# Pairing the 64-row score products of latent attention and retention in the two halves of the TensorE array

## The chip, the cores and the metric

The kernel runs on one core of one Trainium2 chip. The metric is the time of one execution on the device, in microseconds (us); a run is one such time, and the time of a kernel is the median of its runs. The profile is that of one execution, and all its times are counted from the start of its span.

## What is computed

One layer of an encoder for 256 tokens of 1024 features, in float32. After a norm, a wide product with `w_in` feeds four mixers, whose outputs are projected, gated and summed; then come `w_out`, a feed-forward block and a gated projection. Mixers C and D are the ones that matter here:

```python
# C, latent attention: 8 heads; q and k have 128 plain features and 64 rotated ones; k's rotated part is shared
q = (_rms_norm(cq, qa_g) @ wuq).reshape(b, s, 8, 192);  kv = (_rms_norm(ckv, kva_g) @ wukv).reshape(b, s, 8, 256)
k_nope, v = kv[..., :128], kv[..., 128:]
a = softmax(einsum('bhqd,bhkd->bhqk', q, k) * 192 ** -0.5);  y = einsum('bhqk,bhke->bhqe', a, v)
# D, retention: 8 heads, q and k of 64 rotated features, scores times a decay, then a norm per head and a gate
scores = einsum('bhnid,bhnjd->bhnij', q, k) * decay;  y = silu(g) * head_layer_norm(scores @ v)
```

B, differential attention, also has products over 64 features: two score maps for each of its 8 heads.

## The kernel before, in words

Weights are streamed once through the core. Every matrix is split into a high and a low part (`hi` by ScalarE or VectorE, `lo` by VectorE), and each product is made of three matmuls: high by high, high by low, low by high (`mm3`, line 196). The stream (`a_mode`, line 387, and `b_mode`, line 416) loads chunks of up to 1 MB into `raw` (3 buffers, issued on SP's queue at line 362), splits them in pieces into `hi` and `lo` (5 buffers each), and multiplies into the four PSUM banks named `acc`.

The mixers' own work is "side work": Python generators that emit a step at a time between chunks of the stream (`tick`, line 333; at most four generators in turn, each as far as a credit of estimated cost goes). `yield` ends a step. All side work that needs TensorE shares four other PSUM banks, named `mm` (`mm_bank`, line 181): transposes (`pair_T`, line 580), scores and products with v. The framework orders the instructions of each engine at build time from the program's order, the dependences and its own estimate of durations, gives out the buffers, and sets the waits; each engine then runs its list in order.

`c_mix` (line 763) makes a pair of heads of C. After three steps of preparation the pair's operands are in place: `qn`, `kn` (128 rows, high and low, per head) and `pe` (the rotated 64 features: head 0 of the pair in partitions 0 to 63, head 1 in 64 to 127). Then `scores(h)` (line 793) takes one `mm` bank for a head and emits, for each of two tiles of 128 queries, three matmuls over 128 rows and three over 64 rows into the same columns, followed by the softmax: a row maximum and its product with `rq` on VectorE (lines 802, 803), two `Exp` with running sums on ScalarE (line 805), a reciprocal and two scalings on VectorE (lines 807, 809). Head 0 is one step, head 1 the next:

```python
e0 = scores(0)
yield 1.4
e1 = scores(1)
yield 1.4
```

`d_mix` (line 877) does the same for a pair of D: `scores(h)` (line 881) loads a decay table of 256 KB on SP's queue (line 883), makes six matmuls over 64 rows (two tiles of keys, three each) into one `mm` bank and multiplies it by the decay on VectorE (line 890). There are four pairs in C and four in D. `b_mix` (line 631) makes two maps of a head in one step: the comment at line 640 says that they run in the two halves of the array's rows, each into its own bank.

Of the kernel before, what the change touches and what calls it, by code (L numbers as in the profile page):

```python
# [10 lines left out]
AF = mybir.ActivationFunctionType  # L11
ALU = mybir.AluOpType
AX = mybir.AxisListType
# [6 lines left out]
# buffers of each kind of tile  # L20
NR, NY, NG, NL, NS = 5, 8, 4, 18, 16
# side work: generators in turn; its cost for a chunk of weights, by phase
WIDTH = 4
G0, G1, G2, G3 = 3.0, 3.0, 3.5, 2.5
# priority of weight loads and splits over what else is ready; of the first norm over everything
AHEAD, AHEAD_S, FIRST = 60, 60, 100000
# in these pieces of the stream VectorE makes every second high part, as ScalarE has more to do
# [6 lines left out]
# weight streams: (name, first row, rows, first column, columns, mode); a chunk of at most 1 MB is  # L34
# contiguous in each partition. "a": [k][n]; "b": [128-column tile][k][128].
# [61 lines left out]
# then, on every partition: gains of rotated columns [q/k][plain/halves swapped][16 | 64], diff_lam,  # L97
# and rope tables [tile of tokens][diff C 16 | S 16 | mla C 64 | S 64 | ret C 64 | S 64]
# [5 lines left out]
def _pack_params(w):  # L104
    """the small parameters, a column of 128 features or a row for all partitions each"""
    import numpy as np

    out = np.empty((P, N_PAR), np.float32)
    for name, k in _COLS:
        v = np.asarray(w[name][0])  # L110
        if name in ('diff_q_g', 'diff_k_g'):
            v = np.concatenate([np.ones(16, np.float32), v[16:]] * 2)
        elif name in ('mla_q_g', 'mla_k_g'):
            v = v[:P]
        out[:, _COL[name]:_COL[name] + k] = v.reshape(k, P).T
    rows = []
    for dn, mn in (('diff_q_g', 'mla_q_g'), ('diff_k_g', 'mla_k_g')):
        d, m = np.asarray(w[dn][0])[:16], np.asarray(w[mn][0])[P:]
        rows += [d, m, d[8:], d[:8], m[32:], m[:32]]
    rows.append(np.asarray(w['diff_lam'][0]).reshape(-1))  # L120
    out[:, O_GR:O_ROPE] = np.concatenate(rows)[None, :]
    out[:, O_ROPE:] = _rope().reshape(2, P, 288).transpose(1, 0, 2).reshape(P, 576)
    return out


def _pack_lru(w):
    """[256 features][direction] blocks on the diagonal of 128 x 128: [128 c, (a | x), 2, 128 d]"""
# [40 lines left out]
def encoder_kernel(ctx: ExitStack, tc: tile.TileContext, a, out):  # L168
# [26 lines left out]

    def mm3(o, lhsT, rhs, start, stop):
        """the product of two split operands (hi, lo)"""
        mm(o, lhsT[0], rhs[0], start, False)
        mm(o, lhsT[0], rhs[1], False, False)
        mm(o, lhsT[1], rhs[0], False, stop)  # L200
# [4 lines left out]
    def split(hi, lo, src):  # L205
        """src = hi + lo exactly, each part a float32r number"""
        act(hi, src, AF.Copy)
        tt(lo, src, hi.bitcast(F32), SUB)
# [5 lines left out]
    # ---------------------------------------------------------- inputs and constants  # L214
    # x first; then the sum over branches, then the residual stream
# [14 lines left out]
    # the square root's table is in place when x arrives  # L230
# [15 lines left out]
    def derived_params():  # L246
        nc.sync.dma_start(par[:, O_LATE:], a['params'][:, O_LATE:])
        # rope tables times gains; [q/k][C/S][tok tile][16 | 64]
# [12 lines left out]
        # the silu of D comes out doubled  # L261
# [3 lines left out]
        # 8 softplus(-lambda), and its negative  # L265
# [18 lines left out]
    def rsqrt(v, scale, bias, e):  # L284
        """v = (v * scale + bias) ** -0.5 for a small tile; e: -0.5 in its shape"""
# [6 lines left out]
    # ---------------------------------------------------------- norm of whole rows  # L292
# [3 lines left out]
    def rstd(src, scratch):  # L296
        """column: 1 / rms of the rows of src [128, 1024]"""
# [9 lines left out]
    def rows_to_T(src, gname, t, k4):  # L307
        """four 128-column blocks of src [128 tok, 1024], times gains, transposed and split"""
# [9 lines left out]
    # ---------------------------------------------------------- interleaving  # L318
    # side work (generators) is emitted a step at a time between the chunks of the weight streams; a step
    # yields its rough cost to the busier of ScalarE and VectorE  # L320
# [12 lines left out]
    def tick(part):  # L333
        """after this part of a chunk: a step of each generator, as far as the credit goes"""
# [9 lines left out]
    def finish(*gens):  # L344
        """emit the rest of these"""
# [7 lines left out]
    # ---------------------------------------------------------- weight streams  # L353
# [11 lines left out]
    def pieces(raw, o, n, alloc=None):  # L365
        """a split piece of a chunk: n columns of each partition from o on"""
# [20 lines left out]
    def a_mode(xh, xl, name, KT, n0, nn, by_token=0):  # L387
        """tokens on partitions: [128 tok, nn] for each tile of tokens. The last by_token k tiles go
        through for the first tile of tokens before the second."""
# [29 lines left out]
    def b_mode(xh, xl, name, n0):  # L419
        """features on partitions: [128 feat, 2, 256 tok] for 256 columns of a weight, K = 1024"""  # L420
# [16 lines left out]
    with tc.tile_pool(name="br", bufs=1) as br:  # L437
        # tiles of 2 KB a partition: long-lived ones, and those of a step or two
# [23 lines left out]
        def yhl():  # L462
            """split operand in halves of four 128-feature tiles"""
# [8 lines left out]
        def gates(i):  # L472
            """tanh of half the logits, in rows of tokens, {(tile of tokens, half of the features)}:
            1 + tanh(z / 2) = 2 sigmoid(z), in the same table as exp"""
# [10 lines left out]
        def merge(first, gs, y, wname):  # L485
            """twice the sum over branches"""
# [10 lines left out]
        # ------------------------------------------------------ A: gated linear recurrence  # L497
        def a_in(u):
            """features 256 u .."""
# [10 lines left out]
        def a_mix(u, xc, rr):  # L510
            """rr [128 feat, 2, 256 tok]: the sum of both directions' recurrences"""
# [51 lines left out]
        # ------------------------------------------------------ rope in rows of tokens  # L563
        def rope_rows(dst, src, C, Sn, half, shape):
            """dst = rotated src; views [128, ..., 2*half]; C, Sn broadcast to shape"""
# [14 lines left out]
        def pair_T(src):  # L580
            """transposes of [128 tok, 128] blocks: bank [128, 2, 256 tok]"""
# [6 lines left out]
        def y_to_T(y, p, yy, gcol):  # L588
            """y [128 tok, t, 2 heads, 128] -> heads 2p, 2p+1 of yy"""
            split_scaled(*yw(yy, 2 * p), pair_T(lambda t, h: y[:, t, h, :]), gcol)  # L590

        # ------------------------------------------------------ B: differential attention
        def b_in(c):
            """heads 4c .. 4c+3, in pairs"""
# [36 lines left out]
        def b_mix(p, qT, rq, kT, v, yy):  # L631
# [5 lines left out]
            def scores(h):  # L637
                e = [SH("be").rearrange("p (t s) -> p t s", t=2) for _ in range(2)]
                sm = small.tile([P, 2, 2, 2], F32, tag="bsm", name="bsm")
                # the two maps run in the two halves of the array's rows, each into its own bank  # L640
# [46 lines left out]
            # y * r1 * rsqrt(mean((y r1)^2) + eps)  # L687
# [10 lines left out]
        # ------------------------------------------------------ C: latent attention  # L698
        def c_in():
            """latents in rows of tokens: tiles of columns 0.., 256.., 512.. of cq | ckv | kpe"""  # L700
# [10 lines left out]
        def c_lat(cs, cT, sc, kpr):  # L711
            """normed and transposed; the rotated shared part of k and its sum of squares"""
            # sums of squares of cq 0:256, cq 256:384, ckv 0:128, ckv 128:256, kpe
# [28 lines left out]
        def c_proj(hp, cT):  # L742
            """heads 2hp, 2hp+1"""
# [19 lines left out]
        def c_mix(hp, qs, qp, ks, v, sc, kpr, yy):  # L763
# [29 lines left out]
            def scores(h):  # L793
                w = slice(64 * h, 64 * h + 64)
                e = SH("ce").rearrange("p (t s) -> p t s", s=S)
                sm = small.tile([P, 2, 2], F32, tag="csm", name="csm")
                ps = mm_bank().rearrange("p (t s) -> p t s", s=S)
                for t in range(2):
                    ck = slice(t * P, (t + 1) * P)
                    mm3(ps[:, t, :], [x[:, h, ck] for x in qn], [x[:, h, :] for x in kn], True, False)  # L800
                    mm3(ps[:, t, :], [x[w, 0, ck] for x in pe], [x[w, 1, :] for x in pe], False, True)
                nc.vector.tensor_reduce(out=sm[:, :, 0], in_=ps, axis=AX.X, op=MAX, negate=True)
                tt(sm[:, :, 0], sm[:, :, 0], rq[:, :, h], MULT)
                for t in range(2):
                    act(e[:, t, :], ps[:, t, :], AF.Exp, scale=rq[:, t, h:h + 1], bias=sm[:, t, 0:1],
# [12 lines left out]
            e0 = scores(0)  # L818
            yield 1.4
            e1 = scores(1)  # L820
# [10 lines left out]
        # ------------------------------------------------------ D: retention  # L831
        def d_in():
            """q and k: (rotation, transposed) for heads 0..3 and 4..7"""
# [24 lines left out]
        def d_vg(c):  # L858
            """heads 4c .. 4c+3, in pairs"""
# [17 lines left out]
        def d_mix(p, qT, kT, v, sg, yy):  # L877
# [3 lines left out]
            def scores(h):  # L881
                dec = SH("dec").rearrange("p (k s) -> p k s", s=S)
                nc.sync.dma_start(dec, a['decay'][:, 2 * p + h])
                w = slice(64 * h, 64 * h + 64)
                ps = mm_bank().rearrange("p (k s) -> p k s", s=S)
                for k in range(2):
                    mm3(ps[:, k, :], [x[w, p % 2, k * P:(k + 1) * P] for x in kT], [x[w, p % 2, :] for x in qT],
                        True, True)
                st = SH("dst").rearrange("p (k s) -> p k s", s=S)
                tt(st, ps, dec, MULT)  # L890
# [13 lines left out]
            st0 = scores(0)  # L904
            yield 0.7
            st1 = scores(1)
# [14 lines left out]
        # ------------------------------------------------------ the streams in order  # L921
# [66 lines left out]
        # ------------------------------------------------------ after the branches  # L988
# [9 lines left out]
        # the norm's factor of a token comes in after the products: (r relu(z))^2 = r^2 relu(z)^2  # L998
# [39 lines left out]
        for t in range(2):  # L1038
            for c in range(2):
                g = br.tile([P, 512], F32, tag="gate", name="pg", bufs=NG)  # L1040
                # the last bank in halves: the first's way out runs under the second's products
# [32 lines left out]
```

## Time and profile before

| what | value |
|---|---|
| runs (us) | 746.73, 748.01, 746.41; median 746.73 |
| span of the profiled execution | 745.1 us |
| TensorE matmuls (PE) | busy 727.8 us, 98% of the span, 4066 matmuls |
| TensorE weight loads (PEld) | busy 628.8 us, 84% |
| VectorE (DVE) / ScalarE (ACT) | busy 527.8 us, 71% / 428.9 us, 58% |
| GpSimd (POOL) | busy 48.2 us, 6% |
| DMA | 128.47 MB, mean 172 GB/s |

The page gives no time for the profiled execution but its span, which lies 1.6 us below the median of the runs. Matmuls overlap, so a group's busy time and the duration of one matmul say little of what it costs; what counts is the distance from one start to the next, and the timeline has it: there each line is a run of like instructions, with its start, its length and its count. `64*128` in a line is a matmul with 64 rows and 128 columns of stationary operand.

### The profile page before, as it was taken

How to read it: one execution, taken by the hardware profiler on the slowest of the kernel's cores; microseconds unless marked ns; L12 is line 12 of the kernel's file. 1: busy time of each engine (PE TensorE's matmuls, PEld its weight loads, DVE VectorE, ACT ScalarE, POOL GpSimd, SP SyncE). 2: the span in 40 equal slices, each digit the busy share in tenths (PEclk: the TensorE clock that was granted, in tenths of full speed). 3: DMA queues.
4: the chain of work that ended last, by engine and by line, in shares of the span. 5: the costliest groups of instructions: out<-in, count | busy, mean ns of one | idle time of the engine just before them, and what ended most of it. 6: DMA issues, size and time to landing. Idle time of an engine off the chain costs nothing.

```text
span 745.1 us, 10613 instructions
## 1 busy us (share of the span) xinstructions
PE 727.8 (98%) x4066; PEld 628.8 (84%) x4066; DVE 527.8 (71%) x893; ACT 428.9 (58%) x744; POOL 48.2 (6%) x58
## 2 busy tenths in 40 slices
PE   4999999999999999999999999999999999999997
PEld 4988889987888888888888888877899999888886
DVE  5988979998868789866675678566666666446652
ACT  6589867473655994565554344535755555345551
POOL 0000002221020022110000101000000000000000
PEclk9999999999999999999999999999999999999999
DMA  7754443365344454343345355653655545536611
GB/s 295 263 212 170 170 171 141 128 241 184 117 155 135 123 193 170 114 169 128 136 175 198 142 212 203 235 177 107 225 177 195 195 170 174 202 133 226 219 64 57
DMA packets 22802, 128.47 MB, mean 172 GB/s; under 512 B 2656, under 2 KB 2912, under 8 KB 9440
## 3 DMA queue, kind: packets, MB, share of 16 engines
q1 hardware_dynamic: 22752, 127.80, 48.7%
q8 instruction: 32, 0.52, 0.3%
q14 instruction: 18, 0.15, 0.1%
HBM read 126.74 MB, written 1.05 MB: 172 GB/s over the span
## 4 chain that ended last, share of the span: by engine, by line
PE 65%; DVE 1%; ACT 0%; issue 0%
PE acc L194 57%; PE mm L194 5%; PE mm L203 3%; DVE lo L185 0%; DVE gate L188 0%; ACT hi L191 0%; DVE pg L185 0%; DVE xs L185 0%; ACT pg L191 0%
## 5 line engine op out<-in xcount | busy, mean ns | idle before, releaser
L185 DVE TENSOR_TENSOR lo<-raw,hi 128x1024 fp32r<-128x1024 f32 (+3 forms) x226 | 268.8, 1194 | 127.5 <-ACT hi L191 127.0
L191 ACT ACTIVATE hi<-raw 128x1024 fp32r<-128x1024 f32 (+2 forms) x200 | 207.8, 1043 | 196.7 <-PE acc L194 169.1
L194 PE MATMUL acc<-hi,xTh 128*128 128x512 f32 (+3 forms) x376 | 146.5, 390 | 0.0
L194 PE MATMUL acc<-hi,y 128*128 128x512 f32 x448 | 144.8, 398 | 0.0
L194 PE MATMUL acc<-hi,xTl 128*128 128x512 f32 (+3 forms) x376 | 142.8, 380 | 0.0
L194 PE MATMUL acc<-lo,xTh 128*128 128x512 f32 (+3 forms) x376 | 142.7, 379 | 0.0
L194 PE MATMUL acc<-xTh,hi 128*128 128x256 f32 x384 | 109.0, 285 | 0.1
L194 PE MATMUL acc<-xTl,hi 128*128 128x256 f32 x384 | 109.0, 284 | 0.2 <-DVE xTl L188 0.2
L194 PE MATMUL acc<-xTh,lo 128*128 128x256 f32 x384 | 108.5, 284 | 0.0
L194 PEld LDWEIGHTS acc<-hi,y 128*128 128x128 f32 x448 | 84.1, 188 | 19.9
L194 PE MATMUL acc<-lo,y 128*128 128x512 f32 x224 | 88.9, 397 | 0.0
L194 PEld LDWEIGHTS acc<-hi,xTh 128*128 128x128 f32 x376 | 70.7, 188 | 13.3
L194 PEld LDWEIGHTS acc<-hi,xTl 128*128 128x128 f32 x376 | 70.6, 188 | 13.1
L194 PEld LDWEIGHTS acc<-lo,xTh 128*128 128x128 f32 x376 | 70.7, 188 | 12.0
L194 PEld LDWEIGHTS acc<-xTl,hi 128*128 128x128 f32 x384 | 73.9, 192 | 0.8 <-DVE xTl L188 0.6
L194 PEld LDWEIGHTS acc<-xTh,hi 128*128 128x128 f32 x384 | 73.7, 192 | 0.4 <-ACT xTh L191 0.4
L194 PEld LDWEIGHTS acc<-xTh,lo 128*128 128x128 f32 x384 | 73.6, 192 | 0.1
L194 PEld LDWEIGHTS acc<-lo,y 128*128 128x128 f32 x224 | 42.1, 188 | 9.4
L194 PE MATMUL acc<-hi,h 128*128 128x512 f32 x128 | 40.7, 397 | 0.0
L194 PEld LDWEIGHTS acc<-hi,h 128*128 128x128 f32 x128 | 23.9, 188 | 5.6
L194 PE MATMUL acc<-lo,h 128*128 128x512 f32 x64 | 25.3, 396 | 0.0
L194 PE MATMUL acc<-hi,cT 128*128 128x384 f32 (+1 forms) x80 | 24.1, 368 | 0.8 <-ACT cqp L191 0.8
(225 smaller groups left out, 908.4 us busy)
## 6 DMA issues: line engine op xcount, KB each, us to landing
raw<-in_weights_dram SPq DMA_DIRECT2D x104, 1024.0 KB, 4.8
raw<-in_weights_dram SPq DMA_DIRECT2D x6, 512.0 KB, 3.5
raw<-in_weights_dram SPq DMA_DIRECT2D x4, 576.0 KB, 3.8
bd<-in_lru_dram SPq DMA_DIRECT2D x8, 256.0 KB, 5.1
gb<-in_gate_b_dram SPq DMA_DIRECT2D x8, 256.0 KB, 5.2
dec<-in_decay_dram SPq DMA_DIRECT2D x8, 256.0 KB, 5.2
raw<-in_weights_dram SPq DMA_DIRECT2D x2, 768.0 KB, 4.3
raw<-in_weights_dram SPq DMA_DIRECT2D x2, 640.0 KB, 3.7
```

Of the source, the lines that this page charges most:

```text
L185: nc.vector.tensor_tensor(out=o, in0=x, in1=y, op=op)
L191: nc.scalar.activation(o, x, f, **kw)
L194: nc.tensor.matmul(o, lhsT=lhsT, rhs=rhs, start=start, stop=stop)
L203: nc.tensor.transpose(o, x, ident[:x.shape[0], :x.shape[0]])
```

## The change

In C, the matmuls of both heads of a pair are emitted together, ahead of both softmaxes: first the 12 over 128 rows (head 0's six, then head 1's), then the 12 over 64 rows, alternating between the heads at each matmul. Each head has its own `mm` bank, taken at once. Within a bank only the very first matmul carries the start flag, as the two tiles' sums are now open together; `mmg` is `mm` with the framework's check of such groups left out. The softmax of a head (`weigh(h)`) stays where `scores(h)` was, in two steps. In D, both decay tables are loaded first, then the 12 matmuls over 64 rows are emitted, alternating between the heads; the products with the decay stay in two steps. The number of matmuls, loads and other instructions is the same. The rest of the diff removes comments.

```diff
+    def mmg(o, lhsT, rhs, start, stop):
+
+        nc.tensor.matmul(o, lhsT=lhsT, rhs=rhs, start=start, stop=stop, skip_group_check=True)
+
...
-            def scores(h):
-                w = slice(64 * h, 64 * h + 64)
+
+
+            ps = [mm_bank().rearrange("p (t s) -> p t s", s=S) for _ in range(2)]
+            for h in range(2):
+                for t in range(2):
+                    ck = slice(t * P, (t + 1) * P)
+                    for i, j in ((0, 0), (0, 1), (1, 0)):
+                        mmg(ps[h][:, t, :], qn[i][:, h, ck], kn[j][:, h, :], t + i + j == 0, False)
+            for t in range(2):
+                ck = slice(t * P, (t + 1) * P)
+                for i, j in ((0, 0), (0, 1), (1, 0)):
+                    for h in range(2):
+                        w = slice(64 * h, 64 * h + 64)
+                        mmg(ps[h][:, t, :], pe[i][w, 0, ck], pe[j][w, 1, :], False, i == 1)
+
+            def weigh(h):
                 e = SH("ce").rearrange("p (t s) -> p t s", s=S)
                 sm = small.tile([P, 2, 2], F32, tag="csm", name="csm")
-                ps = mm_bank().rearrange("p (t s) -> p t s", s=S)
-                for t in range(2):
-                    ck = slice(t * P, (t + 1) * P)
-                    mm3(ps[:, t, :], [x[:, h, ck] for x in qn], [x[:, h, :] for x in kn], True, False)
-                    mm3(ps[:, t, :], [x[w, 0, ck] for x in pe], [x[w, 1, :] for x in pe], False, True)
-                nc.vector.tensor_reduce(out=sm[:, :, 0], in_=ps, axis=AX.X, op=MAX, negate=True)
+                nc.vector.tensor_reduce(out=sm[:, :, 0], in_=ps[h], axis=AX.X, op=MAX, negate=True)
...
-            e0 = scores(0)
+            e0 = weigh(0)
             yield 1.4
-            e1 = scores(1)
+            e1 = weigh(1)
...
-            def scores(h):
-                dec = SH("dec").rearrange("p (k s) -> p k s", s=S)
-                nc.sync.dma_start(dec, a['decay'][:, 2 * p + h])
-                w = slice(64 * h, 64 * h + 64)
-                ps = mm_bank().rearrange("p (k s) -> p k s", s=S)
-                for k in range(2):
-                    mm3(ps[:, k, :], [x[w, p % 2, k * P:(k + 1) * P] for x in kT], [x[w, p % 2, :] for x in qT],
-                        True, True)
+
+            decs = []
+            for h in range(2):
+                decs.append(SH("dec").rearrange("p (k s) -> p k s", s=S))
+                nc.sync.dma_start(decs[h], a['decay'][:, 2 * p + h])
+            ps = [mm_bank().rearrange("p (k s) -> p k s", s=S) for _ in range(2)]
+            for k in range(2):
+                for i, j in ((0, 0), (0, 1), (1, 0)):
+                    for h in range(2):
+                        w = slice(64 * h, 64 * h + 64)
+                        mm(ps[h][:, k, :], kT[i][w, p % 2, k * P:(k + 1) * P], qT[j][w, p % 2, :], i + j == 0, i == 1)
+
+            def weigh(h):
                 st = SH("dst").rearrange("p (k s) -> p k s", s=S)
-                tt(st, ps, dec, MULT)
+                tt(st, ps[h], decs[h], MULT)
                 return st
```

## Rows read from the trace of the kernel before

**Rows 1.** The page's first part: busy time, share of the span, instructions.

```profile
PE 727.8 (98%) x4066; PEld 628.8 (84%) x4066; DVE 527.8 (71%) x893; ACT 428.9 (58%) x744; POOL 48.2 (6%) x58
```

**Rows 2.** The page's chain that ended last, shares of the span by engine.

```profile
PE 65%; DVE 1%; ACT 0%; issue 0%
```

**Rows 3.** Waits of PE over the span: us in total, times, longest us.

```profile
PE acc L194 <- ACT cqp L191: 0.8, 1, 0.8
...
PE mm L194 <- ACT be L191: 0.4, 1, 0.4
```

**Rows 4.** Windows of C and D: busy us of each engine (instructions), granted clock, DMA.

```profile
270.00:300.00 30.00, 30.00 (x159) 24.74 (x157) 26.92 (x48) 19.75 (x38) 6.40 (x5) 1.00 0.50 175
...
sum 200.00, PE 200.00 PEld 165.95 DVE 147.94 ACT 104.09 POOL 16.81; mean PE 28.57 PEld 23.71 DVE 21.13 ACT 14.87 POOL 2.40
```

**Rows 5.** Waits of ACT, then of SP's queue, 270 to 470 us, longest.

```profile
ACT hi L191 <- PE acc L194: 62.2, 37, 3.6
...
SPq L362 <- DVE lo L185: 149.2, 24, 9.5
```

**Rows 6.** Tile mm, matmuls over 64 rows of C, D: ns min/median/max, first and last start.

```profile
L194 PE MATMUL mm<-cpe x48: 273/278/384, 281.7 to 365.1; 64*128 64x256 f32 x48
L194 PE MATMUL mm<-dqk x48: 275/279/384, 402.7 to 441.6; 64*128 64x256 f32 x48
```

**Rows 7.** Timeline of PE: the two heads of C's first pair (start us, length).

```profile
281.25 0.52 PE L194 MATMUL mm<-ckn,cqn 128*128 128x256 f32 x3
281.70 0.62 PE L194 MATMUL mm<-cpe 64*128 64x256 f32 x3
282.24 0.62 PE L194 MATMUL mm<-ckn,cqn 128*128 128x256 f32 x3
282.79 0.62 PE L194 MATMUL mm<-cpe 64*128 64x256 f32 x3
283.34 0.66 PE L203 MATMUL mm<-ident,cqs 128*128 128x128 f32 x4
...
289.43 0.52 PE L194 MATMUL mm<-ckn,cqn 128*128 128x256 f32 x3
...
291.51 0.66 PE L203 MATMUL mm<-ident,cks 128*128 128x128 f32 x4
```

**Rows 8.** Timeline of PE: D's first pair and the stream behind it.

```profile
402.69 1.69 PE L194 MATMUL mm<-dqk 64*128 64x256 f32 x12
404.31 0.50 PE L194 MATMUL acc<-hi,xTh 128*128 128x512 f32 x1
404.65 0.40 PE L194 MATMUL acc<-lo,xTh 128*128 128x512 f32 x1
404.89 0.40 PE L194 MATMUL acc<-hi,xTl 128*128 128x512 f32 x1
```

**Rows 9.** Timeline of PE: B's maps, one head, then two heads in a row.

```profile
149.90 0.98 PE L194 MATMUL mm<-bT 64*128 64x256 f32 x12
150.82 0.41 PE L194 MATMUL acc<-hi,xTh 128*128 128x320 f32 x1
...
239.47 1.71 PE L194 MATMUL mm<-bT 64*128 64x256 f32 x24
241.10 0.44 PE L194 MATMUL acc<-hi,cT 128*128 128x384 f32 x1
```

**Rows 10.** Timeline of PE: the one head of B with a wait inside.

```profile
244.86 0.62 PE L194 MATMUL mm<-bT 64*128 64x256 f32 x3
245.90 0.97 PE L194 MATMUL mm<-bT 64*128 64x256 f32 x9 [0.41 <-ACT be L191]
246.80 0.50 PE L194 MATMUL acc<-hi,cT 128*128 128x512 f32 x1
```

**Rows 11.** Timeline of ACT: the last Exp of head 0 and of head 1.

```profile
288.36 0.56 ACT L191 ACTIVATE ce<-mm,csm,crq 128x256 f32<-128x256 f32 x1
...
294.88 0.56 ACT L191 ACTIVATE ce<-mm,csm,crq 128x256 f32<-128x256 f32 x1
```

More of the change, by code (lines that the diff above doesn't have):

```diff
@@ L791, in c_mix @@
             yield 1.3
-            def scores(h):
-                w = slice(64 * h, 64 * h + 64)
+            ps = [mm_bank().rearrange("p (t s) -> p t s", s=S) for _ in range(2)]
[11 more added lines that the diff above has]
+            def weigh(h):
                 e = SH("ce").rearrange("p (t s) -> p t s", s=S)
                 sm = small.tile([P, 2, 2], F32, tag="csm", name="csm")
-                ps = mm_bank().rearrange("p (t s) -> p t s", s=S)
-                for t in range(2):
-                    ck = slice(t * P, (t + 1) * P)
-                    mm3(ps[:, t, :], [x[:, h, ck] for x in qn], [x[:, h, :] for x in kn], True, False)
-                    mm3(ps[:, t, :], [x[w, 0, ck] for x in pe], [x[w, 1, :] for x in pe], False, True)
-                nc.vector.tensor_reduce(out=sm[:, :, 0], in_=ps, axis=AX.X, op=MAX, negate=True)
+                nc.vector.tensor_reduce(out=sm[:, :, 0], in_=ps[h], axis=AX.X, op=MAX, negate=True)
                 tt(sm[:, :, 0], sm[:, :, 0], rq[:, :, h], MULT)
                 for t in range(2):
-                    act(e[:, t, :], ps[:, t, :], AF.Exp, scale=rq[:, t, h:h + 1], bias=sm[:, t, 0:1],
+                    act(e[:, t, :], ps[h][:, t, :], AF.Exp, scale=rq[:, t, h:h + 1], bias=sm[:, t, 0:1],
                         accum_out=sm[:, t, 1:2])
@@ L902, in apply @@
                     nc.vector.bn_aggr(mv[:, t, h, :], bn[:, t, :])
-            st0 = scores(0)
+            st0 = weigh(0)
             yield 0.7
-            st1 = scores(1)
+            st1 = weigh(1)
             yield 0.7
```

## The prediction, made before the changed kernel was run

> **What bounds the kernel now.** I read the page's first part first: PE is busy for 98% of the span, the next engine for 71% [rows 1]. As a busy PE may only be a PE with long overlapping matmuls, I then read the chain that ended last: it runs over PE for nearly all that the page prints, and never over a queue [rows 2]. Two views say whether that holds where the change is made. The windows from 270 to 470 us, which hold all of C's and D's scores [rows 6], show PE busy for 200.0 of 200.0 us, at the granted clock 1.00, and VectorE for 147.9 [rows 4]. Of PE's waits, the longest for the stream is of 0.8 us and the one for an `mm` bank of 0.4 us [rows 3], and neither can lie in these 200 us. So whoever shortens PE's list there shortens the kernel, as long as the split weights are there in time. They are: in these 200 us ScalarE waits 62.2 us, in 37 places, for PE to give back a `hi` buffer, and SP's queue waits 149.2 us for `raw` buffers [rows 5]. The stream is ahead of PE, not behind it.
>
> **What a 64-row matmul costs.** The reader should look at distances between starts, not at the 0.28 us that one matmul is said to take [rows 6], since they overlap. D's twelve follow one another: 404.31 - 402.69 = 1.62 us [rows 8]. B's twelve have the same shape, 64x256, and the program puts map 0 into the upper and map 1 into the lower half of the rows: 150.82 - 149.90 = 0.92 us [rows 9]. Two heads of B in a row, 24 matmuls, take 241.10 - 239.47 = 1.63 us [rows 9]. So twelve more cost 0.71 us, which is 0.118 us for two, and a block carries a fixed 0.92 - 0.71 = 0.21 us. Taken off D's block that leaves (1.62 - 0.21) / 12 = 0.118 us for one. A pair in the two halves costs what a single one costs: half of the time is saved.
>
> **What changing between 128 and 64 rows costs.** C's first head shows it [rows 7]. Three matmuls at 0.118 would be 0.35 us. The first three (128 rows, the stream before them has 128 too) take 281.70 - 281.25 = 0.45, so 0.10 is paid on the way into 64 rows. Each later group of three, with a change on both sides, takes 0.54 to 0.55: 0.19 more than its products. The first matmul of the stream behind a 64-row block takes 0.34 where the next takes 0.24 [rows 8]: again 0.10. One excursion from 128 rows to 64 and back thus costs 0.10 + 0.19 + 0.10 = 0.39, say 0.38 us (twice 0.19). C makes two in a head, sixteen in all.
>
> **The change part by part.**
>
> *C, order.* The pair's 12 matmuls over 128 rows stand together, then the 12 over 64 rows: one excursion where there were four. 3 x 4 pairs = 12 fewer, 12 x 0.38 = 4.6 us, all on PE's list and so on the path.
>
> *C, pairing.* 48 matmuls over 64 rows [rows 6] become 24 pairs: 24 x 0.118 = 2.8 us. No row shows pairs that add to sums which 128-row matmuls have just written. Nearest below is B's block (0.92), nearest above D's unpaired one (1.62); a loss beyond that is excluded, as C's own 64-row groups already add to such sums at 0.54 a group, fixed part included [rows 7]. I take B's, being the only row of the same arrangement (two banks, two halves, same shape). Check by blocks: before, a pair takes 283.34 - 281.25 = 2.09 and 291.51 - 289.43 = 2.08 [rows 7] plus twice 0.10 behind it, 4.37 us; after, 12 x 0.118 + 0.10 + 0.92 + 0.10 = 2.54. That is 1.83 less, four times 7.3, against 4.6 + 2.8 = 7.4.
>
> *D, pairing.* D's two heads already stand in one block of twelve [rows 8], with no excursion to save. Paired it should take 0.92 for 1.62: 0.70 x 4 pairs = 2.8 us. That the program alternates at each matmul where B has three and three should not matter: B's block is as short as six pairs though its program has no two matmuls of a pair side by side. Bounds: 0 and 2.8; I take 2.8.
>
> Here the Trainium skill can be weighed (TensorE: Matmul & The Clock Gate, "Measured speedup vs the span model"): a pack of matmuls in different row groups spans the duration of one plus about 4 ns for each further one. If packs followed each other without overlap, my estimate from that rule and the 0.28 us of rows 6 is 6 x 0.282 = 1.69 us for twelve, no gain at all, and the whole change would give 743.5 us. The rows of B say 0.92, so here packs do overlap, and the trace decides.
>
> *What moves without a price.* Head 1's 12 matmuls of C go a step earlier, from 289.43 to behind head 0's [rows 7]; PE's total is the same but for the terms above, and the 2.5 us that now stand in one place between stream matmuls delay no split, as the split pieces are ahead. The softmaxes stay in their steps, on VectorE and ScalarE, as many as before. D's second decay table is asked for together with the first; SP's queue has the `raw` loads behind it, and it waits for 149.2 of 200 us on full buffers [rows 5]. No instruction and no DMA is added; the start flags and the left-out check are no instructions. If the cover went (a split piece late by d), PE would wait d once for that piece.
>
> *Sum.* 4.6 + 2.8 + 2.8 = 10.2 us. The profiled span of 745.1 becomes 734.9; the median of the runs lies 1.6 above that span, so 746.7 - 10.2 = 736.5 us.
>
> **Rivals.**
>
> *The pairs don't overlap.* The list could come out as head 0's six, then head 1's, as D's block shows today [rows 8]. Then only C's excursions are saved: 746.7 - 4.6 = 742.1 us. For it: two heads' products on one list are no proof of overlap. Against it: every block of B runs at the pair's pace [rows 9], and the new program alternates. Chance 0.08.
>
> *Part of it is kept.* VectorE is busy for 26.9 of the first 30 us [rows 4], and ScalarE makes its `hi` only as fast as the side work lets it; with two heads' scores ready at once, both softmaxes may push a split back. The first pair's 1.8 us could then be lost: 738.3 us. A block broken by a late bank, as one of B's is, costs 246.80 - 244.86 = 1.94 for 0.92, so 1.0 us [rows 10]; two of these among the eight give 738.5 us, both things together 740.3. Chance 0.17.
>
> *The bank held longer, slower than before.* The place is PE's list behind a pair of C: head 1's `mm` bank is now taken with head 0's, while its softmax stays a step later. Head 0's last `Exp` ends at 288.36 + 0.56 = 288.9, head 1's at 294.88 + 0.56 = 295.4 [rows 11], so one more of the four banks is held for up to 8.2 us a pair (289.43 - 281.25). If a transpose that needs that bank stands early on PE's list, PE waits with the stream behind it. It decides from 10.2 / 4 = 2.6 us a pair, or 2.9 for slower by over 0.2%; at 5.4, midway between 2.6 and 8.2, it gives 736.5 + 4 x 5.4 = 758.1 us. For it: B, which takes two banks at once, has the one bank wait of the trace, 0.41 us [rows 10]. Against it: that is the only one in eight heads of B [rows 3], and the build places the transposes with the banks in view. Chance 0.04. The Trainium skill (TensorEngine Tiling (Array Packing), "Restrictions and Gotchas") warns of the same, that row tiling raises the pressure on PSUM; the trace agrees in kind, with that one wait of 0.41 us.
>
> **How the numbers follow.** The forecast has 0.71 and gives 736.5; its own range is 735.2 to 737.8, from 0.02 us on each of 12 excursions, 0.05 on each of 8 blocks and the spread of the runs (0.3 below the median, 1.3 above). To hold eight in ten the range goes up through the partial case, to 740.3, and down to 735.0; both ends of the pairing's price beyond that (742.1) are left to the 0.08. A measurement of this kernel can tell some 0.2%, 1.5 us, from no change. Faster by more than that hold the forecast, the partial case and the first rival: 0.71 + 0.17 + 0.08 = 0.96, less 0.02 for several partial losses that add up to 9 us. The slower case has 0.04; some 0.01 of it is a wait near the point where gain and loss cancel. That makes 0.94 faster, 0.03 the same, 0.03 slower.
>
> **What would show it.** In the timeline of PE, C's pair should be one group of 12 matmuls `mm<-ckn,cqn` followed by 12 `mm<-cpe`, four times, the first about 1.5 us long from start to start and the second 0.9; D's groups of 12 should go from 1.62 to 0.9. PE should still be busy for all but a fraction of the windows of C and D, and its total should fall by about 10 us; its waits should stay under 2 us beyond the start. The stream's weights, VectorE and ScalarE should show the same busy times. Wrong would be: 12 `mm<-dqk` still in 1.6 us (no overlap); 64-row groups of three or six with others between them (the order was not kept); or new waits of PE on `ce`, `csm` or `dst` (the banks), or on `lo` (the stream).

## The result, and the profile after

The changed kernel takes 736.94 us (median of 4 runs, 736.32 to 737.41) beside 746.57 us for the kernel before (4 runs, 746.37 to 748.01): a ratio of 0.9867, interval 0.9855 to 0.9878, 9.6 us less. The span of the profiled execution went from 745.1 to 735.1 us.

The page's first part, to be read against [rows 1]:

```profile
PE 718.0 (98%) x4066; PEld 622.7 (85%) x4066; DVE 526.6 (72%) x893; ACT 428.2 (58%) x744; POOL 49.4 (7%) x58
```

The counts are the same and so is the work of VectorE and ScalarE; PE is busy for 9.8 us less, and still for 98% of the span. Nothing else became the bound.

The timeline of PE at C's first pair (start us, length; to be read against [rows 7]):

```profile
280.92 1.60 PE L198 MATMUL mm<-ckn,cqn 128*128 128x256 f32 x12
282.45 0.98 PE L198 MATMUL mm<-cpe 64*128 64x256 f32 x12
283.35 0.66 PE L207 MATMUL mm<-ident,cqs 128*128 128x128 f32 x4
```

One group of 12 over 128 rows (282.45 - 280.92 = 1.53 us from start to start), one of 12 over 64 rows (0.90 us): the pair's scores are done 2.43 us after they began, where the two heads took 2.09 and 2.08 us. All four pairs of C have this form.

The same view at D's four pairs (against [rows 8]):

```profile
394.52 0.39 PE L194 MATMUL acc<-lo,xTh 128*128 128x512 f32 x1
394.75 0.39 PE L194 MATMUL acc<-hi,xTl 128*128 128x512 f32 x1
395.07 1.70 PE L194 MATMUL mm<-dqk 64*128 64x256 f32 x24
396.69 0.50 PE L194 MATMUL acc<-hi,xTh 128*128 128x512 f32 x1
...
423.31 0.98 PE L194 MATMUL mm<-dqk 64*128 64x256 f32 x12
424.22 0.50 PE L194 MATMUL acc<-hi,y 128*128 128x512 f32 x1
424.56 0.39 PE L194 MATMUL acc<-lo,y 128*128 128x512 f32 x1
424.79 0.61 PE L194 MATMUL acc<-hi,y 128*128 128x512 f32 x2
425.63 1.63 PE L194 MATMUL mm<-dqk 64*128 64x256 f32 x12 [0.22 <-DVE y L188]
427.19 0.50 PE L194 MATMUL acc<-lo,y 128*128 128x512 f32 x1
```

The first two pairs stand in one block of 24 and take 1.62 us together, what one pair took before. The third takes 0.91 us. The fourth does not go as forecast: it was pulled ahead, close behind the third, PE waits 0.22 us for VectorE to finish with `y` (the transposed outputs of the first two pairs, which hold two `mm` banks), and then its twelve take 1.56 us, almost unpaired. VectorE's row:

```profile
424.83 1.40 DVE L188 SCALAR_TENSOR_TENSOR y<-mm,gng,y 128x512 fp32r<-128x512 f32 x2
```

These are two operations, one for each bank. In the trace the first ends at 425.57 us, and head 0's scores begin at 425.63; the second ends at 426.23, and head 1's begin at 426.28. By then five of head 0's six have started without a partner.

**A measure that leaves the ends out.** The executions differ by about 1 us in when the first transposes can start, and in the last steps. For C and D alone I take the distance from the first score matmul of C to the last group of transposes of D's output (`mm<-ident,dy`), called the stage. Its end is this row (the first four of that group), of the kernel before and then of the changed one:

```profile
462.17 0.60 PE L203 MATMUL mm<-ident,dy 128*128 128x128 f32 x4
```

```profile
452.16 0.60 PE L207 MATMUL mm<-ident,dy 128*128 128x128 f32 x4
```

The stage took 462.17 - 281.25 = 180.92 us [rows 7] and takes 452.16 - 280.92 = 171.24: 9.68 us of the 10.0 by which the spans differ arose there, and nothing of it was given back later.

### The profile page after: what moved, and what is told of

The parts are those of the page before. It is cut to its first block, busy times and chain, and to the rows that moved or that the text cites. A ratio compares the mean times of both kernels' runs of the same rounds, so it can differ in the third digit from the quotient of the medians.

```text
span 735.1 us, 10616 instructions
## 1 busy us (share of the span) xinstructions
PE 718.0 (98%) x4066; PEld 622.7 (85%) x4066; DVE 526.6 (72%) x893; ACT 428.2 (58%) x744; POOL 49.4 (7%) x58
## 4 chain that ended last, share of the span: by engine, by line
PE 64%; DVE 1%; ACT 0%; issue 0%
PE acc L194 57%; PE mm L194 3%; PE mm L207 2%; PE mm L198 1%; ACT hi L191 0%; DVE lo L185 0%; DVE gate L188 0%; DVE pg L185 0%; DVE y L188 0%; DVE xs L185 0%; ACT pg L191 0%
```

## The experiments

Three theories were set against each other over the runs: that changing between 128 and 64 rows costs 0.38 us an excursion and pairing saves 0.118 us a pair; that only the pairing pays; and that banks held longer make PE wait. Where a stage is given, its first and last row are the ones named above; the numbers beside it are these two starts.

**C alone, and D alone.** The changed kernel with D's functions put back, then with C's put back.

> C as in the changed kernel, D as before. Theory (excursions to 64 rows at 0.38 us each, twelve fewer, 4.6; 24 pairs at 0.118, 2.8): 7.4 us off 746.6, 739.2 us; groups of 12 mm<-cpe in 0.9 us. Rival (the change of row mode costs little, only the pairing pays): C and D have 24 pairs each, so C would carry half of the 9.6 us measured, 741.8 us.

Measured: 739.58 us (739.06 to 740.12), ratio 0.9908 [0.9893, 0.9923]. Stage 454.41 - 280.73 = 173.68 us, 7.24 less than before, where the first theory had 7.4 and the second about 4.8.

> D as in the changed kernel, C as before. Theory: the two profiles' D blocks differ by 2.3 us (one pair's pairing is broken), so 744.3 us, and up to 2.8 less than 746.6, 743.8, if no pair is broken. Rival (only the pairing pays): half of 9.6, 741.8 us.

Measured: 744.51 us (743.76 to 745.17), ratio 0.9971 [0.9959, 0.9984]. Stage 459.76 - 281.21 = 178.55 us, 2.37 less, near the 2.3 expected; its fourth pair is broken in the same way. The parts add up: 7.24 + 2.37 = 9.61 of the 9.68 measured together. C and D have 24 pairs each, but C gives three times what D gives, so the pairing can't be the whole of it.

**One excursion more in each pair of C.**

```diff
-            for h in range(2):
-                for t in range(2):
-                    ck = slice(t * P, (t + 1) * P)
+            for t in range(2):
+                ck = slice(t * P, (t + 1) * P)
+                for h in range(2):
...
-            for t in range(2):
-                ck = slice(t * P, (t + 1) * P)
                 for i, j in ((0, 0), (0, 1), (1, 0)):
                     for h in range(2):
```

> The changed kernel with C's matmuls ordered by tile of queries: six of 128 rows, six of 64 rows in pairs, and again, so two excursions a pair instead of one; all else the same. Theory: 4 more excursions at 0.38 us, 1.5 us more than the changed kernel, 738.4 us. Rival (the change of row mode costs little): 736.9 us, no change.

Timeline of PE of this kernel, C's first pair:

```profile
280.87 0.88 PE L198 MATMUL mm<-ckn,cqn 128*128 128x256 f32 x6
281.67 0.62 PE L198 MATMUL mm<-cpe 64*128 64x256 f32 x6
282.22 0.97 PE L198 MATMUL mm<-ckn,cqn 128*128 128x256 f32 x6
283.12 0.62 PE L198 MATMUL mm<-cpe 64*128 64x256 f32 x6
283.68 0.44 PE L207 MATMUL mm<-ident,cqs 128*128 128x128 f32 x2
```

The pair takes 283.68 - 280.87 = 2.81 us instead of 2.43: the same 24 matmuls, still paired, cost 0.38 us more for one more excursion. Stage 453.64 - 280.87 = 172.77, 1.53 more than in the changed kernel (four times 0.38 is 1.52). The runs give 739.01 us (738.63 to 739.88), 2.1 above the changed kernel, which was not run beside it. The first theory stands: order alone, with nothing removed, is worth this. Nor is it the price of adding to sums that other matmuls have just written. D's block shares its sums with nobody and pays on both sides as well: in the changed kernel the last stream matmul before it takes 395.07 - 394.75 = 0.32 us from start to start where the one ahead takes 0.23, and the first behind it 397.03 - 396.69 = 0.34.

**Six and six in C.** D as before, and C's 64-row matmuls in the program one head after the other.

```diff
-                for i, j in ((0, 0), (0, 1), (1, 0)):
-                    for h in range(2):
-                        w = slice(64 * h, 64 * h + 64)
+            for h in range(2):
+                w = slice(64 * h, 64 * h + 64)
+                for t in range(2):
+                    ck = slice(t * P, (t + 1) * P)
+                    for i, j in ((0, 0), (0, 1), (1, 0)):
...
```

> C grouped as in the changed kernel, but its 64-row matmuls in the program as head 0's six, then head 1's six; D as before. Theory (no overlap, as in D's block of the kernel before): only the excursions are saved, 4.6 us, 742.0 us, and groups of 12 mm<-cpe take 1.62 us. Rival (TensorE looks far enough ahead to pair them by itself, as it does with B's three and three): 739.2 us, like C alone, and 0.91 us a group.

```profile
282.61 1.32 PE L198 MATMUL mm<-cpe 64*128 64x256 f32 x12
283.86 0.44 PE L207 MATMUL mm<-ident,cqs 128*128 128x128 f32 x2
```

Neither expectation came: 741.05 us (740.58 to 741.67), and the group takes 283.86 - 282.61 = 1.25 us, between 0.91 and 1.62. The 0.37 us saved are three pairs. TensorE does start matmuls of the other half ahead of earlier ones in its list, here three ahead: head 1's first three run beside head 0's last three, and the rest of both run alone; the single starts in the trace show it. (That each engine runs its list in order, as was said of the kernel before, does not hold for these.) The build didn't reorder the list instead: in the trace the last matmul of a bank raises TensorE's semaphore, by one where it directly follows another such matmul in the list and by more otherwise. In C head 1's raises it by one in the changed kernel, which alternates, and by more than one here and in the next run. Stage 456.12 - 281.08 = 175.04, 5.88 less than before: 4.6 for the excursions and 4 x 0.37 = 1.5 for the pairs make 6.1.

**Three and three in C and D.** The order in which B's program has its maps.

```diff
-                for i, j in ((0, 0), (0, 1), (1, 0)):
-                    for h in range(2):
-                        w = slice(64 * h, 64 * h + 64)
+                for h in range(2):
+                    w = slice(64 * h, 64 * h + 64)
+                    for i, j in ((0, 0), (0, 1), (1, 0)):
...
```

> The changed kernel with the 64-row matmuls of C and D in the program as three of head 0, three of head 1, for each tile, as B has them, not alternating at each matmul. Theory (TensorE pairs three and three by itself, as B shows): 736.9 us as the changed kernel, groups of 12 mm<-cpe in 0.91 us. Rival (the alternation in the program is what pairs them): 736.9 + 2.8 + 2.3 = 742.0 us, 1.62 us a group.

```profile
282.60 0.98 PE L198 MATMUL mm<-cpe 64*128 64x256 f32 x12
283.51 0.44 PE L207 MATMUL mm<-ident,cqs 128*128 128x128 f32 x2
```

737.3 us (one run), 0.91 us a group, stage 452.38 - 281.07 = 171.31, 0.07 more than with the heads in turn. At three and three the alternation isn't needed; TensorE makes the pairs.

**The same half for both heads.**

```diff
-                        w = slice(64 * h, 64 * h + 64)
+                        w = slice(0, 64)
...
```

> The changed kernel with head 0's 64 rows taken for both heads in C's and D's 64-row products: head 1's scores are computed from head 0's rotated features, in the same half of the array. Order, banks, shapes and counts stay. Theory (the halves are what lets two run at once): pairing lost, 12 mm<-cpe in 1.62 us, 24 mm<-dqk in 3.0 us, 736.9 + 2.8 + 2.3 = 742.0 us. Rival (two banks in turn are enough): 736.9 us.

Timelines of PE, C's first and D's first block:

```profile
282.03 1.69 PE L198 MATMUL mm<-cpe 64*128 64x256 f32 x12
283.65 0.44 PE L207 MATMUL mm<-ident,cqs 128*128 128x128 f32 x2
...
397.59 3.13 PE L194 MATMUL mm<-dqk 64*128 64x256 f32 x24
400.65 0.50 PE L194 MATMUL acc<-hi,xTh 128*128 128x512 f32 x1
```

Order, banks and counts are those of the changed kernel, yet the twelve take 1.62 us and the twenty-four 3.06. 741.37 us (one run), stage 456.66 - 280.51 = 176.15, 4.91 more. So the two halves of the rows are what lets two run at once, and with two banks in the same half there is no gain. For C alone the rows give the pairing 4 x (1.62 - 0.91) = 2.84 us; of the 7.24 measured with C alone that leaves 4.40 for the twelve excursions, 0.37 each.

**D's two products with the decay in one step.**

```diff
             st0 = weigh(0)
-            yield 0.7
             st1 = weigh(1)
-            yield 0.7
+            yield 1.4
```

> The changed kernel with both of D's products with the decay in the step of the scores, so that both banks of a pair come free at once. Theory (the fourth pair of D was broken by a bank that came late): its block and wait lose about 0.9 us, and with pairs three and four in one block one excursion, 0.4 us, goes too: 735.6 us. Rival (the broken block is chance, or the gain is lost elsewhere): 736.9 us.

> The changed kernel once more, on the same chip and in the same rounds as the run before it, to compare the two: 736.9 us, both theories.

```profile
422.95 1.70 PE L194 MATMUL mm<-dqk 64*128 64x256 f32 x24
424.58 0.50 PE L194 MATMUL acc<-hi,y 128*128 128x512 f32 x1
```

735.49 us (735.11 to 736.39) beside 736.89 (736.38 to 738.15) for the changed kernel in the same rounds, 1.4 less; against the kernel before 0.9853 [0.9837, 0.9870] and 0.9871 [0.9856, 0.9885]. Pairs three and four now stand in one block of 24 in 1.63 us and wait for nothing. By the rows that is 0.65 for the broken block, 0.22 for the wait and about 0.4 for one excursion. The edit moved more than the release of the banks, though: the transposes that hold the two banks of `y` now start at 416.39, 6.6 us ahead of the block, where they stood 1.0 us ahead of the third pair. Which of the two ended the wait was not tried apart. This is the fastest version measured, and a small change to the changed kernel.

**Six and six in D**, with both banks taken at once, to see whether the wait in PE's list ends TensorE's reach.

> The changed kernel with D's products in the program as six of head 0, then six of head 1, both banks taken at once. Theory (TensorE reaches about three matmuls ahead into the other half, as the run with six and six in C showed, 1.25 us a group): 12 mm<-dqk in about 1.25 us, 24 in about 2.3, the whole some 1 us above the changed kernel, 738 us. Rival (the wait on head 1's first weight load, which D's list has and C's has not, ends the reach, as in D's block before): 12 in 1.62 us, 24 in 3.1, 739 us.

```profile
395.12 2.04 PE L194 MATMUL mm<-dqk 64*128 64x256 f32 x24
397.09 0.50 PE L194 MATMUL acc<-hi,xTh 128*128 128x512 f32 x1
...
423.70 1.32 PE L194 MATMUL mm<-dqk 64*128 64x256 f32 x12
424.95 0.50 PE L194 MATMUL acc<-hi,y 128*128 128x512 f32 x1
```

1.25 us for twelve, as the theory had it, but 1.97 for twenty-four where it had 2.3, and 737.25 us (one run) where it had 738. The mechanism is the theory's and its count was short: three pairs form at each handover from one head to the other, and the block of 24 has three handovers ((3.06 - 1.97) / 0.12 is nine pairs), not two. The fourth pair is broken as in the changed kernel, with 1.50 us. A wait in the list does not by itself end the reach: in the fourth pair of the changed kernel head 1's first matmul is the second in the list and waits for its bank, and four of head 0's listed behind it started first. What stays open: in the kernel before, D's block has the same order and no overlap at all, 1.62 us [rows 8]. There head 1's bank was taken by a later step; what its first load waits for was not tried.

**Three `mm` banks instead of four**, in the changed kernel and in the one before (`bufs=3` for that pool).

> The changed kernel with three mm banks instead of four. Theory (the fourth bank only matters where two pairs of D, or two heads of B, stand close together): some pairs of B and D broken, C's groups intact, 1 to 3 us slower than with four, 738 to 740 us. Rival (two banks held by a pair of C starve the rest, and PE waits): more than 6 us slower, over 743 us, and more lost than by the kernel before with three banks.

> The kernel before with three mm banks instead of four, to set beside the changed kernel with three. Theory: some heads of B broken, 0 to 2 us slower, 746.6 to 748.6 us. Rival: as much lost as the changed kernel loses, then the loss is not due to pairs holding two banks.

742.29 us (742.11 to 743.40) and 750.79 (749.89 to 751.26), where the kernel before with four took 747.44 in the same rounds. Both expectations for the first were off: it loses about 4.6 us (742.29 less 0.987 x 747.44), neither 1 to 3 nor over 6. The kernel before loses 3.35, more than the 0 to 2 expected. Timeline of PE in the changed kernel with three banks, a head of B, then a pair of C:

```profile
155.37 0.62 PE L194 MATMUL mm<-bT 64*128 64x256 f32 x3
156.88 0.97 PE L194 MATMUL mm<-bT 64*128 64x256 f32 x9 [0.89 <-ACT be L191]
157.79 0.41 PE L194 MATMUL acc<-hi,xTh 128*128 128x320 f32 x1
...
299.95 2.03 PE L198 MATMUL mm<-ckn,cqn 128*128 128x256 f32 x12
301.91 0.98 PE L198 MATMUL mm<-cpe 64*128 64x256 f32 x12
```

B's part is the same in both kernels: such a head takes 2.42 us for 0.92, and from B's first map to C's first scores the loss is 2.1 us in each (133.44 for 131.33, and 133.40 for 131.35). Of C's four pairs one pays 0.4 us (1.96 for 1.6). The stages: 457.49 - 284.19 = 173.30, 2.06 more than with four banks, and for the kernel before 465.16 - 283.47 = 181.69, 0.77 more. Even starved of a bank, the change keeps 8.4 of its 9.7 us there. Pairs do need the bank, for 2.06 - 0.77 = 1.3 us in all, but not so badly that PE would wait for several us.

**C's two softmaxes in one step as well.**

```diff
             e0 = weigh(0)
-            yield 1.4
             e1 = weigh(1)
-            yield 1.4
+            yield 2.8
...
```

> The run with D's two products with the decay in the step of the scores, and C's two softmaxes in one step as well. Theory (C's banks keep nobody waiting, and VectorE and ScalarE have room): the same as with D's alone, 735.5 us, within 0.7. Rival (the second softmax at once pushes split pieces back): new waits of PE on lo or hi, 737 us or more.

736.85 us (736.41 to 737.19), ratio 0.9863 [0.9848, 0.9878]: not the 735.5 expected, and no better than D's alone; on another chip, with intervals that overlap, the two can't be told apart. No wait for `lo` or `hi` appears, one of 0.4 us on `ce` does, so neither side was shown.

## Why the prediction was right

The forecast was 736.5 us and 736.94 was measured; the sum was 10.2 us and the stage gave 9.7. One piece of arithmetic does not come out: 0.02 on each of 12 excursions and 0.05 on each of 8 blocks make 0.64, and with 0.3 below and 1.3 above that is 735.6 to 738.4, not the forecast's own 735.2 to 737.8. The result lies in either.

*What bounds the kernel* held. With less on its list PE is as full as before. The window of C and D in the changed kernel, 280 to 460 us (busy us of PE, PEld, DVE, ACT, POOL):

```profile
280.00:460.00 180.00, 179.78 (x952) 150.74 (x951) 137.38 (x255) 93.44 (x156) 15.60 (x19) 1.00 0.51 178
```

PE idles for 0.22 us, the one wait before D's fourth pair. The cover named for the moved work held too; in that window ScalarE still waits 59.2 us, 36 times, for PE to give back `hi`:

```profile
ACT hi L191 <- PE acc L194: 59.2, 36, 4.6
```

*C, order* (4.6 us) and *C, pairing* (2.8): 7.4 in the sum, 7.24 measured with C alone, of which the rows give the pairing 2.84 and leave 4.40 for the order. The price of an excursion, worked out as 0.38 from the rows before, came out as 0.38 a pair where one was added. B's block as the price of pairs that add to earlier sums was the right end of the bounds: 0.90 us, not 1.62.

*D, pairing* was the term that was mis-sized: 2.8 forecast, 2.37 measured. The first three pairs do what was forecast; the fourth gave its gain back to a wait for a bank (0.22) and a broken block (1.56 - 0.91 = 0.65). That is the forecast's partial case, once instead of twice. One excursion saved by the merging of pairs one and two, about 0.4 us that the forecast didn't have, made up for part of it, which was luck: 2.8 - 0.87 + 0.4 is 2.3.

*The first rival* (no overlap) fell with 0.90 us a group; what it feared is real in a milder form, as six and six shows, and the program's order avoids it. *The slower case* rested on head 1's bank being held 8.2 us longer, since its softmax stays a step later. It isn't held so long. In the changed kernel's timeline of ScalarE head 1's first and last `Exp` are

```profile
288.96 0.56 ACT L191 ACTIVATE ce<-mm,csm,crq 128x256 f32<-128x256 f32 x1 [0.35 <-DVE csm L185]
...
289.52 0.55 ACT L191 ACTIVATE ce<-mm,csm,crq 128x256 f32<-128x256 f32 x1
```

and end at 290.1, not at 295.4 as before [rows 11]: with the scores there, the build moved head 1's softmax up next to head 0's, and the bank came free 5.3 us sooner than the rival had it. All four pairs show it: from head 0's last `Exp` to head 1's it was 6.5 to 10.7 us before and is 1.1 to 2.4. A related wait did come in D, where a pair needs two banks that the transposes still hold; it cost 0.9 us in all.

## What to carry to other kernels

Where TensorE is full, look for matmuls over half of its rows: price them by the distance between starts, once alone and once beside a partner in the other half, and price each passage into and out of them as well, which here brought more than the pairing (4.4 against 2.8 us in C). Group them so that there are few passages, and put the two halves at most three matmuls apart in the list: one and three apart all pairs formed, six apart only half, and nothing between was tried. Every pair takes two PSUM banks at once, so look at who holds them when the pair is due: a block that waits for its second bank loses the pairing too. Consuming both banks in the step that fills them went with 1.4 us less in D; doing so in C as well showed no further gain.

## What had not been expected of the hardware

TensorE makes pairs out of order, with a reach of about three: twelve matmuls in the order three and three took 0.91 us, six and six 1.25, all in the same half 1.62. Where head 1's first matmul waited for its bank, in D's fourth pair, head 0's next four started ahead of it. How far the reach goes was not measured beyond these orders. The Trainium skill (TensorE: Matmul & The Clock Gate, "The mechanism") says that matmuls start and end strictly in the order of the program; three and three at the pace of pairs is not in keeping with that, nor are the starts in the trace of six and six, and here the measurement decides.
